# Rotary embedding, one core: the first tile's load cut into eight strided transfers

What was changed: tile 0 arrives in eight transfers instead of two, each of every eighth partition with one 64 KB run per DMA engine; and the load of tile 2 is split 10 and 6 rows around the first store instead of 8 and 8.

## Chip, cores, metric

One core of one Trainium2 chip. The metric is device time in microseconds. For a single core a lone run is reported with the state "unknown"; where that is so, I say so.

## The reference, cut

```python
x: (16, 512, 16, 64) float32   # batch, seq, heads, dim: 33.55 MB
cos, sin: (512, 32) float32
x1, x2 = x[..., :32], x[..., 32:]
first  = x1[..., :16] * cos[..., :16] - x1[..., 16:] * sin[..., :16]
second = x1[..., :16] * sin[..., :16] + x1[..., 16:] * cos[..., :16]
out = concatenate([first, second, x2], -1)
```

Half of each row is rotated and half is only copied. Everything is read once and written once: 67.1 MB.

## The kernel before

Four tiles of 8.39 MB, each [128 partitions x 16 rows x 4 KB], so 64 KB per partition, pass through a ring of three buffers. VectorE rotates in place; loads and stores are issued by the sync engine in program order.

```python
K = 16; NS = 3; KC = K // 2; K0 = K // 4
ring = const_pool.tile([P, NS, K, H, D], fp32)

def rows(t, lo, hi):
    return ring[:, t % NS, lo:hi].rearrange("p k h d -> p (k h d)")
def load(t, lo=0, hi=K):
    nc.sync.dma_start(out=rows(t, lo, hi), in_=xf[t, :, lo * R : hi * R])
def store(t, lo=0, hi=K):
    nc.sync.dma_start(out=of[t, :, lo * R : hi * R], in_=rows(t, lo, hi))

# cos and sin: two small loads on GpSimd's queue    [cut]
load(0, 0, K0)
load(0, K0, K)
load(1)
load(2, 0, KC)
# four copies that build the tables on VectorE       [cut]
def rotate(t, lo, hi):
    # mul (b = x1*s), mul (x1 = x1*c), sub, add      [cut]

rotate(0, 0, K0)
rotate(0, K0, (K0 + K) // 2)
rotate(0, (K0 + K) // 2, K)
store(0)
load(2, KC, K)
load(3)                       # same buffer as tile 0: waits for store(0)
for t in range(1, T):
    rotate(t, 0, KC)
    rotate(t, KC, K)
    store(t)
```

Of the kernel before, what the change touches and what calls it, by code (L numbers as in the profile page):

```python
# [1 line left out]

# [4 lines left out]


@with_exitstack
def kernel(  # L10
    ctx: ExitStack,
    tc: tile.TileContext,
    x: bass.AP,
    cos: bass.AP,
    sin: bass.AP,
    out: bass.AP,
):
    nc = tc.nc
    fp32 = mybir.dt.float32
    P = 128  # L20
    B, S, H, D = x.shape
    Q = D // 4
    HF = D // 2



    K = 16
    T = B * S // (P * K)
    PB = S // K
    REP = P // PB  # L30
    R = H * D
    NS = 3
    KC = K // 2
    K0 = K // 4

    xf = x.rearrange("b s h d -> (b s h d)").rearrange("(t p f) -> t p f", t=T, p=P)
    of = out.rearrange("b s h d -> (b s h d)").rearrange("(t p f) -> t p f", t=T, p=P)
    cosf = cos.rearrange("(p k) j -> p (k j)", k=K)
    sinf = sin.rearrange("(p k) j -> p (k j)", k=K)

    const_pool = ctx.enter_context(tc.tile_pool(name="const", bufs=1))
    b_pool = ctx.enter_context(tc.tile_pool(name="bp", bufs=1, space=bass.MemoryType.PSUM))


    ring = const_pool.tile([P, NS, K, H, D], fp32)
    stage = const_pool.tile([PB, 2, K, HF], fp32)
    table = const_pool.tile([P, 2, K, 2, Q], fp32)
# [9 lines that stand above are left out]

    nc.gpsimd.dma_start(out=stage[:, 0].rearrange("p k j -> p (k j)"), in_=cosf)  # L58
    nc.gpsimd.dma_start(out=stage[:, 1].rearrange("p k j -> p (k j)"), in_=sinf)  # L59
    load(0, 0, K0)  # L60
    load(0, K0, K)
    load(1)
    load(2, 0, KC)


    for r in range(REP):
        nc.vector.tensor_copy(  # L67
            out=table[r * PB : (r + 1) * PB].rearrange("p t k c j -> p (t k) c j"),
            in_=stage.rearrange("p t k j -> p (t k) j")[:, :, 0:Q]
            .unsqueeze(2)  # L70
            .to_broadcast((PB, 2 * K, 2, Q)),
        )
    C = table[:, 0].rearrange("p k c j -> p k (c j)")
    Sn = table[:, 1].rearrange("p k c j -> p k (c j)")

    def rotate(t, lo, hi):
        n = hi - lo
        x1 = ring[:, t % NS, lo:hi, :, 0:HF]
        c = C[:, lo:hi].unsqueeze(2).to_broadcast((P, n, H, HF))
        s = Sn[:, lo:hi].unsqueeze(2).to_broadcast((P, n, H, HF))  # L80
        b_full = b_pool.tile([P, KC, H, HF], fp32, name="b_t")
        b_t = b_full[:, 0:n]
        nc.vector.tensor_mul(out=b_t, in0=x1, in1=s)  # L83
        nc.vector.tensor_mul(out=x1, in0=x1, in1=c)  # L84
        nc.vector.tensor_sub(  # L85
            out=x1[:, :, :, 0:Q], in0=x1[:, :, :, 0:Q], in1=b_t[:, :, :, Q:HF]
        )
        nc.vector.tensor_add(  # L88
            out=x1[:, :, :, Q:HF], in0=x1[:, :, :, Q:HF], in1=b_t[:, :, :, 0:Q]
        )  # L90

    rotate(0, 0, K0)
    rotate(0, K0, (K0 + K) // 2)
    rotate(0, (K0 + K) // 2, K)
    store(0)
    load(2, KC, K)
    load(3)
    for t in range(1, T):
        rotate(t, 0, KC)
        rotate(t, KC, K)  # L100
        store(t)


# [1 line left out]
_INS = ['x', 'cos', 'sin']  # L105
_OUTS = [((16, 512, 16, 64), 'float32')]


# [23 lines left out]
```

## Time and profile before

| | before |
|---|---|
| median (3 runs, 161.78 to 161.93) | 161.9 us |
| span of the profiled run | 160.1 us |
| hardware DMA queue busy, share of 16 engines | 97.8% |
| VectorE busy | 69% |
| mean rate | 420 GB/s |
| one 64 KB run on one DMA engine | 2.418 us |

A "run" in this document is the contiguous stretch that one DMA engine moves for one partition. The trace has a record of each run with start and duration; no view prints them, so where I quote run times they come from these records. A record names no engine: that a run belongs to this or that engine is inferred from one run's end meeting the next one's start. The tables by stage stand beside them as a rough check: they count a run with all its bytes in the stretch in which it starts, so a share can exceed 1 and a rate be too high where runs cross the end of a stretch. The prediction below shows the views themselves.

### The profile page before, as it was taken

To read this page: it belongs to the slowest core of one execution; us is meant where nothing else is said; L and a number is where in the kernel's file an instruction comes from. 1 tells how busy PE (TensorE), PEld (TensorE's weight loads), DVE (VectorE), ACT (ScalarE), POOL (GpSimd) and SP (SyncE) were. 2 spreads that over 40 slices of the span, in tenths; PEclk is the share of its full clock that TensorE was granted. 3 is DMA by queue.
4 is the path that set the end of the run, shared out by engine and by line. 5 is a ranking of instruction groups with operands and counts; after the bars stand their busy time and mean duration, and the time that the engine had idled before them with its cause. 6 is when DMAs were issued, how large, how long until landed. Compare 5 with 4: busy or idle time off the path is not lost.

```text
span 160.1 us, 109 instructions
## 1 busy us (share of the span) xinstructions
DVE 110.0 (69%) x40; POOL 1.3 (1%) x6
## 2 busy tenths in 40 slices
DVE  0069709999999999999999994799999900000000
POOL 3000000000000000000000000000000000000000
DMA  6999999699699799899996996996996996996991
GB/s 197 385 504 454 393 459 524 262 524 491 295 401 581 328 524 409 377 393 418 483 540 295 491 524 262 524 524 262 524 524 262 524 524 262 524 491 295 524 459 66
DMA packets 1504, 67.24 MB, mean 420 GB/s; under 512 B 192, under 2 KB 192, under 8 KB 224
## 3 DMA queue, kind: packets, MB, share of 16 engines
q1 hardware_dynamic: 1440, 67.11, 97.8%
q0 software_dynamic: 64, 0.13, 0.2%
HBM read 33.69 MB, written 33.55 MB: 420 GB/s over the span
## 4 chain that ended last, share of the span: by engine, by line
DMA 50%; DVE 28%; DVEq 1%; issue 0%; SPq 0%
DMA ring<-in_x_dram 32%; DMA out_dram<-ring 18%; DVE b_t L83 10%; DVE ring L84 10%; DVE ring L85 5%; DVE ring L88 3%; DVEq L127 1%; SPq L53 0%; DVEq L83 0%
## 5 line engine op out<-in xcount | busy, mean ns | idle before, releaser
L83 DVE TENSOR_TENSOR b_t<-ring,table 128x4096 f32<-128x4096 f32 (+2 forms) x9 | 35.6, 3959 | 8.2 <-DMA ring<-in_x_dram 8.0
L84 DVE TENSOR_TENSOR ring<-ring,table 128x4096 f32<-128x4096 f32 (+2 forms) x9 | 35.6, 3950 | 0.3
L85 DVE TENSOR_TENSOR ring<-ring,b_t 128x2048 f32<-128x2048 f32 (+2 forms) x9 | 18.4, 2049 | 0.3
L88 DVE TENSOR_TENSOR ring<-ring,b_t 128x2048 f32<-128x2048 f32 (+2 forms) x9 | 18.4, 2042 | 0.0
L67 DVE COPY table<-stage 32x1024 f32<-32x1024 f32 x4 | 2.7, 684 | 9.2 <-DMA stage<-in_sin_dram 9.1
L58 POOL DMA_DIRECT2D stage<-in_cos_dram x1 | 0.6, 631 | 0.8 <-PEq L127 0.8
L59 POOL DMA_DIRECT2D stage<-in_sin_dram x1 | 0.5, 498 | 0.0
L116 POOL MEMSET const-bfloat16-1.0<- 128x1 bf16 x1 | 0.1, 102 | 0.0
L116 POOL MEMSET const-float32-0.0<- 128x1 f32 x1 | 0.1, 99 | 0.2 <-issue 0.2
L116 POOL MEMSET const-float32-1.0<- 128x1 f32 x1 | 0.1, 99 | 0.0
L116 POOL MEMSET const-uint8-127<- 128x1 uint8 x1 | 0.1, 99 | 0.0
## 6 DMA issues: line engine op xcount, KB each, us to landing
ring<-in_x_dram SPq DMA_DIRECT2D x2, 4096.0 KB, 43.9
ring<-in_x_dram SPq DMA_DIRECT2D x1, 6144.0 KB, 22.4
ring<-in_x_dram SPq DMA_DIRECT2D x1, 2048.0 KB, 8.5
stage<-in_cos_dram POOLq DMA_DIRECT2D x1, 64.0 KB, 6.0
stage<-in_sin_dram POOLq DMA_DIRECT2D x1, 64.0 KB, 7.2
out_dram<-ring SPq DMA_DIRECT2D x4, 36.4
ring<-in_x_dram SPq DMA_DIRECT2D x2, 35.0
```

The lines of the kernel that those rows point to most:

```text
L58: nc.gpsimd.dma_start(out=stage[:, 0].rearrange("p k j -> p (k j)"), in_=cosf)
L59: nc.gpsimd.dma_start(out=stage[:, 1].rearrange("p k j -> p (k j)"), in_=sinf)
L67: nc.vector.tensor_copy(out=table[r * PB : (r + 1) * PB].rearrange("p t k c j -> p (t k) c j"), in_=stage.rearrange("p t k j -> p (t k) j" ...
L83: nc.vector.tensor_mul(out=b_t, in0=x1, in1=s)
L84: nc.vector.tensor_mul(out=x1, in0=x1, in1=c)
L85: nc.vector.tensor_sub(out=x1[:, :, :, 0:Q], in0=x1[:, :, :, 0:Q], in1=b_t[:, :, :, Q:HF])
L88: nc.vector.tensor_add(out=x1[:, :, :, Q:HF], in0=x1[:, :, :, Q:HF], in1=b_t[:, :, :, 0:Q])
L116: nc = _bacc.Bacc("TRN2", target_bir_lowering=False, num_devices=1)
L127: with _tile.TileContext(nc) as tc:
```

## The change

Its intent is presumably to bring every DMA engine to 64 KB runs at once and to give each transfer all 16 engines. VectorE can then not start on the first four rows, and the 10/6 split keeps the queue filled until the later first store.

```diff
-    K0 = K // 4
+    K2 = 10
+    G = 8
...
-    load(0, 0, K0)
-    load(0, K0, K)
+    for g in range(G):
+        nc.sync.dma_start(
+            out=ring[:, 0].rearrange("(e g) k h d -> g e (k h d)", g=G)[g],
+            in_=xf[0].rearrange("(e g) f -> g e f", g=G)[g],
+        )
     load(1)
-    load(2, 0, KC)
+    load(2, 0, K2)
...
-    rotate(0, 0, K0)
-    rotate(0, K0, (K0 + K) // 2)
-    rotate(0, (K0 + K) // 2, K)
+    rotate(0, 0, KC)
+    rotate(0, KC, K)
     store(0)
-    load(2, KC, K)
+    load(2, K2, K)
```

The scratch tile of `rotate` is also allocated at its exact size; every piece is now 8 rows, so this changes nothing. The order of instructions on VectorE differs only by the missing third piece of tile 0.

More of the change, by code (lines that the diff above doesn't have):

```diff
@@ L80, in rotate @@
         s = Sn[:, lo:hi].unsqueeze(2).to_broadcast((P, n, H, HF))
-        b_full = b_pool.tile([P, KC, H, HF], fp32, name="b_t")
-        b_t = b_full[:, 0:n]
-        nc.vector.tensor_mul(out=b_t, in0=x1, in1=s)
+        b_t = b_pool.tile([P, n, H, HF], fp32, name="b_t")
+        nc.vector.tensor_mul(out=b_t[:], in0=x1, in1=s)
         nc.vector.tensor_mul(out=x1, in0=x1, in1=c)
```

## The prediction

In the prediction the sum of the forecast came to 161.9 + 19.3 - 0.9 = 180.3 us: the time before; 19.3 us because the eight runs of tile 0 on each engine were to take twice their 2.418 us, 4.84; and 0.9 us less for the tidying and the start. The doubling was my supposition, no trace of the kernel before showed it. "It" in "Nothing downstream gives it back" and "the 19.3" are this term. Rival A is tile 0 at half rate, B is tile 0 at full rate.

> **What bounds the kernel now.** I read the page first (engine busy shares, slices, DMA queues), then the chain of waits, then the sync engine's own waits, then a table of stages.
>
> ```profile
> DVE 110.0 (69%) x40; POOL 1.3 (1%) x6
> q1 hardware_dynamic: 1440, 67.11, 97.8%
> q0 software_dynamic: 64, 0.13, 0.2%
> HBM read 33.69 MB, written 33.55 MB: 420 GB/s over the span
> ring<-in_x_dram SPq DMA_DIRECT2D x1, 6144.0 KB, 22.4
> ring<-in_x_dram SPq DMA_DIRECT2D x1, 2048.0 KB, 8.5
> ```
>
> The hardware DMA queue is busy for 97.8% of all 16 engines' span, VectorE for 69%. So the bound is bytes through the DMA engines: 33.55 MB in, 33.55 MB out. The chain that ended last names VectorE for 28%, and that misleads: while the chain follows VectorE from 23.66 to 44.14 us, the DMA engines are working off loads already queued, and nothing is lost.
>
> The first stage of the timeline and the table by stage:
>
> ```profile
> 11.94 2.30 DVE L83 TENSOR_TENSOR b_t<-ring,table 128x2048 f32<-128x2048 f32 x1
> ...
> 23.66 3.37 DVE L83 TENSOR_TENSOR b_t<-ring,table 128x3072 f32<-128x3072 f32 x1 [4.71 <-DMA ring<-in_x_dram]
> ...
> 44.14 0.35 SPq L56 DMA_DIRECT2D out_dram<-ring  x1
> ```
>
> ```profile
> 0.00:1.75 1.75, 0.00 (x0) 0.70 (x5) 1.00 0.00 0
> 1.75:8.30 6.55, 0.00 (x0) 0.63 (x2) 1.00 1.14 408
> 8.30:22.90 14.60, 9.68 (x8) 0.00 (x0) 1.00 1.04 450
> 22.90:158.60 135.70, 100.33 (x32) 0.00 (x0) 1.00 0.99 427
> 158.60:160.10 1.50, 0.00 (x0) 0.00 (x0) 1.00 0.00 0
> ```
>
> Columns of the second fence: stretch, its length, busy time of VectorE and GpSimd, clock, DMA share, GB/s. The first byte moves at 1.75 us, the last at 158.6, and in between there is no hole.
>
> The trace also holds one record per DMA run, which no view prints. A 64 KB run takes 2.418 us on its engine (27.1 GB/s; 16 engines give 433.6 GB/s), a 48 KB run 1.82 us, a 32 KB run 1.21 us. A 16 KB run takes 0.611 us when undisturbed, but 1.0 to 1.5 us as the first of its engine. Each engine carries 64 times 64 KB: 64 x 2.418 = 154.8 us. From 1.75 to 158.6 are 156.9 us, so all inefficiency of the stream together is 2.1 us. Nearly all of it lies in tile 0, whose last run ends at 23.1 us: 23.1 - 1.75 = 21.35 us against 8 x 2.418 = 19.34.
>
> [...]
>
> [...] each table is a transfer of only 32 partitions, and the 64 software-queue packets are, per table, 16 packets of 4,096 B (two 2 KB rows[...]) and 16 semaphore writes. The 1440 hardware packets are 10 transfers x (128 runs + 16 semaphore writes)[...].
>
> [...]
>
> [...]
>
> [...]
>
> **The change part by part.**
>
> *Bytes, VectorE, tables.* The same 67.1 MB. VectorE loses one group of four operations: tile 0 went in 4+6+6 rows, now 8+8. Before: 2.30 + 2.29 + 1.22 + 1.21 and twice 3.37 + 3.36 + 1.75 + 1.75, together 27.5 us. After: twice 4.43 + 4.42 + 2.29 + 2.28, together 26.8. VectorE can no longer start on 4 rows at 11.94 but waits for the whole tile. With tile 0 down at about 22.5 it would be rotated at 22.5 + 26.8 = 49.3 us instead of 44.14.
>
> *The 10/6 split.* It pays for that. Queued ahead of the first store are now 8 + 8 + 5 = 21 runs of 64 KB per engine, until 1.75 + 1 + 21 x 2.418 = 53.5 us, against 52.2 now. The store issued at 49.3 needs about 1 us to start (0.74 issued, 1.75 first byte, at the start of the span), so 3 us of slack remain. The other end: 6 rows are 6/16 x 19.34 = 7.3 us of transfer between the end of store 0 and the start of load 3, which waits for that store; an issue of about 1 us fits. No bubble at either end: 0 us.
>
> *Eight issues.* Four load issues took 1.88 us of the sync queue, so about 0.45 each; eight take 3.6 us, while one run lasts at least 2.418. The engines stay fed: 0 us. Extra semaphore writes: 7 more per engine at 9 ns, 0.06 us.
>
> *Run length.* 16 + 48 KB become 64 KB: 0.611 + 1.82 = 2.43 against 2.418, times 8: -0.1 us. Of the 2.0 us of excess in tile 0 the first-run latency and the tables' 0.3 us stay; disturbed small runs may go. I estimate -0.8 us.
>
> [...] Nothing downstream gives it back, as every later transfer already runs end to end. Tile 0 would end near 41.5 us, be rotated at 68.3, and the queue would hold work until 41.5 + 13 x 2.418 = 72.9. So no bubble is added to the 19.3 either.
>
> [...]
>
> **The rivals.**
>
> *A, [...]:* 180.3 us (178 to 182). [...]
>
> *B, [...]:* tile 0 runs at full rate and only the tidying remains, 161.9 - 0.8 = 161.1 us (160.4 to 162.5[...]). For it: rate per engine is all the trace shows. After the first table packet the next two 16 KB runs together took about 1.43 us instead of 1.22 on nearly every engine alike[...]. This hints at a cost on the engine's side.
>
> *C, something between:* [...] engines are chosen by partition after all, so that two groups of eight run side by side with the second starting 2 us later. 163 to 174 us.
>
> *D, a new bubble* before store 0 since VectorE starts later: the 3 us of slack speak against it. If the tables came very late (10 us later), VectorE still has them before tile 0 is down.
>
> A gain of over 2% needs 158.7 us. The stream's whole inefficiency is 2.1 us and part of it stays, so that is all but excluded.
>
> **Range and chances.** A gets about 0.62, C 0.06 (most of it beyond 2%), B 0.31. Slower: 0.67, same: 0.32, faster: 0.01. Since A and B lie far apart, a range that holds the time 8 times in 10 has to reach from B's to A's: 160.6 to 182.0 us. The point is A's, 180.3 us, as the likelier one.
>
> **What would show it.** For A: the GB/s of the slices from 4 to 40 us near 215 instead of 440; tile 0's transfers ending one 4.8 us after the other; first multiply at 128x4096 near 41 us; store 0 issued near 68 us; from there on the same spacing of transfers as before (19.35 us per tile), and one 64 KB run of tile 0 about 4.8 us instead of 2.418. For B: first multiply near 22.5 us, store 0 issued near 49.3, last byte near 158. For D: a hole in the DMA row of the slices around 50 us. [...] if runs of tile 0 take 2.42 us, A falls whatever else holds. If they take 4.8 us but the end is less than 17 us later, my claim that nothing downstream gives time back is the faulty step.

## The result

| | before | after |
|---|---|---|
| median | 161.9 us (161.69 to 162.19, 6 runs) | 182.66 us (182.52 to 182.89, 6 runs) |
| span of the profiled run | 160.1 us | 180.9 us |
| last run of tile 0 ends | 23.10 us | 44.04 us |
| last run of the last store ends | 158.6 us | 179.7 us |

The ratio is 1.1283 (95% interval 1.1268 to 1.1297); a ratio here is the mean time of one kernel's fast runs over the mean of the other's of the same rounds, so not quite the ratio of the medians.

The page of the kernel after, engines and queues:

```profile
DVE 109.5 (60%) x36; POOL 1.3 (1%) x6
q1 hardware_dynamic: 1408, 67.11, 97.6%
HBM read 33.69 MB, written 33.55 MB: 372 GB/s over the span
```

The bytes are the same and the queue is as busy as before, 97.6% against 97.8%, but it moves 372 GB/s instead of 420. This is the point to learn from: "busy" counts the time that runs take, and a run that crawls is as busy as one that flies. The shares alone would not say that anything is wrong with the DMA. The page's rate in 40 equal slices of the span does, here before and after:

```profile
GB/s 197 385 504 454 393 459 524 262 524 491 295 401 581 328 524 409 377 393 418 483 540 295 491 524 262 524 524 262 524 524 262 524 524 262 524 491 295 524 459 66
GB/s 232 246 232 174 101 217 217 232 232 232 464 464 464 368 435 435 386 464 464 464 313 435 440 435 464 464 464 464 449 333 391 449 464 464 464 464 449 319 391 232
```

The first ten slices of the second line, 45 us, stay between 101 and 246.

The table by stage of the kernel after (stretch, length, VectorE, GpSimd, clock, DMA share, GB/s):

```profile
2.10:44.10 42.00, 2.73 (x4) 0.27 (x1) 1.00 1.04 226
44.10:179.70 135.60, 106.73 (x32) 0.00 (x0) 1.00 0.98 425
```

All of the loss lies in the first line. Its 226 GB/s and its share of 1.04 include 16 runs of tile 1 that start before 44.10 us; tile 0's own 8.39 MB from 2.10 to 44.04 us are 200 GB/s, against 393 before (1.75 to 23.10 us). From its end on the kernel runs at 425 GB/s, against 427 in the corresponding stretch of before.

The timeline of the kernel after, VectorE's first multiply and the first store:

```profile
0.74 4.99 SPq L63 DMA_DIRECT2D ring<-in_x_dram  x8
...
44.72 4.43 DVE L87 TENSOR_TENSOR b_t<-ring,table 128x4096 f32<-128x4096 f32 x1 [23.16 <-DMA ring<-in_x_dram]
...
71.61 0.35 SPq L57 DMA_DIRECT2D out_dram<-ring  x1
```

VectorE starts at 44.72 us and the store is issued at 71.61 us (the prediction had 41 and 68), while the queue still has loads until 75.6, so no bubble came: the 10/6 split did its part. The eight issues took 4.99 us, not the 3.6 I had worked out, also without harm.

The records of the runs: for g = 0 to 7 a 64 KB run took 4.81, 5.08, 5.06, 5.09, 4.91, 5.11, 5.11 and 5.10 us on the mean of the 16 engines. In the kernel before it takes 2.418. The fifth is a little faster. In e8 below, where two tiles come in this way, the fifth, ninth and thirteenth transfers took 4.93 us a run. What makes them faster is not shown.

### The profile page after: what moved, and what is told of

The parts are those of the page before. It is cut to its first block, busy times and chain, and to the rows that moved or that the text cites. A ratio compares the mean times of both kernels' runs of the same rounds, so it can differ in the third digit from the quotient of the medians.

```text
span 180.9 us, 115 instructions
## 1 busy us (share of the span) xinstructions
DVE 109.5 (60%) x36; POOL 1.3 (1%) x6
## 3 DMA queue, kind: packets, MB, share of 16 engines
q1 hardware_dynamic: 1408, 67.11, 97.6%
## 4 chain that ended last, share of the span: by engine, by line
DVE 54%; DMA 22%; issue 5%; SPq 2%; DVEq 1%
DMA ring<-in_x_dram 22%; DVE b_t L87 20%; DVE ring L88 20%; DVE ring L92 9%; DVE ring L89 6%; SPq L63 2%; DVEq L130 1%; DVEq L87 0%
## 5 line engine op out<-in xcount | busy, mean ns | idle before, releaser
L87 DVE TENSOR_TENSOR b_t<-ring,table 128x4096 f32<-128x4096 f32 x8 | 35.5, 4433 | 23.4 <-DMA ring<-in_x_dram 23.2
L88 DVE TENSOR_TENSOR ring<-ring,table 128x4096 f32<-128x4096 f32 x8 | 35.4, 4425 | 0.3
L89 DVE TENSOR_TENSOR ring<-ring,b_t 128x2048 f32<-128x2048 f32 x8 | 18.3, 2286 | 0.3
L92 DVE TENSOR_TENSOR ring<-ring,b_t 128x2048 f32<-128x2048 f32 x8 | 18.2, 2279 | 0.0
```

What stands on the lines that cost most here:

```text
L87: nc.vector.tensor_mul(out=b_t[:], in0=x1, in1=s)
L88: nc.vector.tensor_mul(out=x1, in0=x1, in1=c)
L89: nc.vector.tensor_sub(out=x1[:, :, :, 0:Q], in0=x1[:, :, :, 0:Q], in1=b_t[:, :, :, Q:HF])
L92: nc.vector.tensor_add(out=x1[:, :, :, Q:HF], in0=x1[:, :, :, Q:HF], in1=b_t[:, :, :, 0:Q])
```

## The experiments

Theories at the start: **P**, the partitions that a transfer covers set its rate: runs that engines move at once to or from certain partitions hold each other up (my supposition). **H**, reading rows 512 KiB apart in HBM is slow. **F**, a small transfer of one run per engine has a fixed cost of about 2.7 us (5.11 - 2.42). All edits below are against the kernel after, unless said otherwise.

| experiment | tile 0's transfers | us per 64 KB run | median us |
|---|---|---|---|
| change | 8 x 16 partitions, step 8 | 5.1 | 182.66 |
| e1 | 1 x 128 | 2.42 | 162.03 |
| e3 | as change, rows together in HBM | 5.1 | 182.5 |
| e5 | 8 x 16, step 2 | 5.1 | 182.71 |
| e4 | 8 x 16, step 1 | 9.3 | 216.77 (one run) |
| e6 | 4 x 32, step 4 | 2.42 | 162.45 |
| e10 | 4 x 32, step 1 | 5.1 | 182.74 (one run) |
| e14 | 2 x 64, step 2 | 2.42 | 162.38 (one run) |
| e15 | 2 x 64, step 1 | 5.1 | 182.79 (one run) |
| e11 | 7 x 16, step 7, and 16 in a block | 3.4 to 4.7; 8.2 (medians by transfer) | 182.73 |

The kernel before took 161.83 to 162.04 us (medians) beside these.

### One transfer for tile 0

```diff
-    for g in range(G): ...        # eight transfers
+    load(0)
```

> Tile 0 arrives in one transfer of 128 partitions, the rest of the change (tile 2 split 10 and 6, halves of 8 rows) stays. All three theories of the loss, P [...], H (rows 512 KiB apart in HBM) and F (a fixed cost of each small transfer), put it into the eight transfers: 161.1 us expected, 160.4 to 162.0. If the rest of the change carried part of the loss, this stays above 163.

162.03 us (161.73 to 162.47, 6 runs) against 161.83; ratio 1.0013 (0.9992 to 1.0034). So the whole loss is in the eight transfers. The rest of the change is worth nothing: my 0.8 us of tidying did not come, and 162.03 is just outside the expected range. The stretch of tile 0, to set against the 226 GB/s of the change:

```profile
1.80:22.90 21.10, 2.73 (x4) 0.57 (x2) 1.00 1.06 441
```

### Only the eight transfers

Against the kernel before:

```diff
-    load(0, 0, K0)
-    load(0, K0, K)
+    for g in range(8): ...        # the eight transfers
```

> The kernel before, with only tile 0's two loads replaced by the eight transfers; tile 2 still split 8 and 8, tile 0 rotated in 4, 6 and 6 rows. P, H and F all expect the loss of the whole change, 182.7 us (182.2 to 183.5). Tile 0 would be rotated near 44.7 + 27.5 = 72.2 us and the queue has work until 44.0 + 12 x 2.418 = 73.0, so with about 1 us to start a store a bubble is just avoided or a few tenths long.

185.45 us (185.13 to 185.67), outside the range: 2.8 us slower than the whole change. The runs of tile 0 are the same (4.86 to 5.12 us), but the loads in the queue ended between 72.55 and 73.24 us and the store was issued at 72.52 and began to move at 73.36, so engines stood idle for 0.1 to 0.8 us. By the records the last runs of the first store and of the load of tile 3 took 3.15 and 3.33 us instead of 2.42 as well, some 1.6 us more; why, I did not test. It shows an idle stretch that the change, with its 10/6 split, does not have; how much of the 2.8 us the split alone is worth, it does not show.

### Near rows in HBM

```diff
-            in_=xf[0].rearrange("(e g) f -> g e f", g=G)[g],
+            in_=xf[0, 16 * g : 16 * g + 16],      # wrong result on purpose
```

> Wrong result on purpose: the eight transfers go to the same partitions 8e+g as in the change, but read 16 rows that lie together in HBM (64 KiB apart instead of 512). P: [...] 182.7 us, a run of tile 0 5.11 us; if the distance in HBM gives the part beyond doubling (5.11 instead of 4.84), 180.5 us and 4.84. H: the loss goes, about 161.5 us and 2.42 a run. F: 182.7 us.

182.5 us, 5.1 us a run. H is out, both as the cause of the loss and as the cause of the part beyond doubling. The 512 KiB pitch costs about 0.2 us (182.66 - 182.5) or nothing.

### Sixteen partitions side by side

```diff
-            out=ring[:, 0].rearrange("(e g) k h d -> g e (k h d)", g=G)[g],
-            in_=xf[0].rearrange("(e g) f -> g e f", g=G)[g],
+            out=ring[16 * g : 16 * g + 16, 0].rearrange("p k h d -> p (k h d)"),
+            in_=xf[0, 16 * g : 16 * g + 16],
```

> Eight transfers of 16 partitions next to each other (16g to 16g+15), rows together in HBM, result right. P: [...] a run takes 9.7 us (4 x 2.418) to 10.2 (twice 5.11), tile 0 ends at 79 to 84 us, the whole 219 to 224 us. H: about 161.5 us. F: as the change, 5.11 us a run and 182.7 us.

216.77 us (one run, state unknown), 9.28 us a run, a little below the range. The table by stage of this run:

```profile
2.00:78.00 76.00, 2.73 (x4) 0.38 (x1) 1.00 0.94 115
78.00:214.00 136.00, 106.74 (x32) 0.00 (x0) 1.00 0.98 424
```

Neighbouring partitions instead of every eighth, and about half the rate again: 115 GB/s instead of 226, or by tile 0's own bytes 111 instead of 200. A fixed cost per transfer (F) cannot do this, as number and size of the transfers are those of the change. A run takes 9.28 / 2.418 = 3.84 times as long as in the kernel before, in the change 5.11 / 2.418 = 2.11 times: near four and two, but not exactly.

### Step 2 instead of step 8

```diff
+        q, b = g // 2, g % 2
-            out=ring[:, 0].rearrange("(e g) k h d -> g e (k h d)", g=G)[g],
-            in_=xf[0].rearrange("(e g) f -> g e f", g=G)[g],
+            out=ring[32 * q : 32 * q + 32, 0].rearrange("(e b) k h d -> b e (k h d)", b=2)[b],
+            in_=xf[0, 32 * q : 32 * q + 32].rearrange("(e b) f -> b e f", b=2)[b],
```

> Eight transfers of 16 partitions with a step of 2 (32q + 2e + b), rows 128 KiB apart in HBM, result right. [...] P: again about double, [...] the whole 178.9 to 182.7 us. H: between 162 and 170 us, as the rows are closer. F fell with the step-1 run (216.8 us).

182.71 us, 5.11 us a run. Other partitions, 2 apart instead of 8, and the same time. It also says that 5.11 us does not need partitions that lie 32 apart in one transfer: here a transfer has none.

### Four transfers of 32 partitions, step 4

```diff
-    for g in range(G):      # and g=G in both rearranges
+    for g in range(4):      # and g=4
```

> Four transfers of 32 partitions, every fourth one (4i+g), so two rows per engine [...]. [...] 162 us. If [...] an engine takes rows 2e and 2e+1 one after the other: [...] 5.1 us a run, about 182.7 us. If rows are dealt out another way (e and e+16): [...] again about 182 us.

162.45 us, 2.42 us a run but for the start and the tables. So it is not the stride over partitions and not the number of transfers. For the two ways of dealing rows to engines that I had named I had expected 182 to 183 us; how the rows are dealt is not in the records, and it stays open.

### Two queues

```diff
+    for i in range(G):
+        g, eng = i // 2 + 4 * (i % 2), (nc.sync, nc.scalar)[i % 2]
+        eng.dma_start(...)        # the same eight transfers
```

> The same eight transfers, issued in turn by the sync queue (g = 0..3[...]) and by ScalarE's queue (g = 4..7[...]). If an engine works one run at a time and all take the two queues in the same order, [...] 180 to 183 us. If each engine keeps a run of either queue in flight or the engines fall out of step, [...] 162 to 166 us, runs that overlap on one engine. P allows either, but only P lets this change anything: the bytes, rows and sizes are the same.

182.0 us (181.78 to 182.31). In the records 16 runs of one queue and 16 of the other follow in turn, 4.9 to 5.2 us each on the mean, so each engine seems to take one run from either queue in turn, all in step. With two queues transfers of g = 0 to 3 and of g = 4 to 7 were on offer at once, and no time was won.

### Tile 1 in eight transfers too

```diff
-    load(1)
+    for g in range(G): ...        # as for tile 0, with ring[:, 1] and xf[1]
```

> Tile 1 comes in eight such transfers as well. P: [...] nothing downstream returns it, so it comes a second time: 8 x (5.11 - 2.42) = 21.5 us more, less some tenths at the seam, 203.5 to 204.5 us. If part of the loss was a start-up cost: under 202. If slack later on returned some: under 202 as well.

231.9 us, far off. The runs of tile 1 took 5.1 us like those of tile 0, and its last run ended at 84.6 us, 40.6 after tile 0's, so the loss did come a second time (40.6 - 19.35 = 21.2 us). Most of the other 28 us is a fault of the experiment, seen in its timeline:

```profile
85.39 4.43 DVE L91 TENSOR_TENSOR b_t<-ring,table 128x4096 f32<-128x4096 f32 x1 [67.69 <-DMA ring<-in_x_dram]
```

VectorE's first multiply on tile 0 waited for tile 1 as well, and by the records no data moved for 9.0 us before the first store, 7.3 us after it and 8.8 us before the last one, 25 us together. As a dose test it is spoiled; the half dose below took its place.

### Step 7

```diff
+    for g in range(7):     # partitions 7e + g of the first 112
+        ...rearrange("(e g) ... -> g e ...", g=7)[g]
+    # one transfer for partitions 112 to 127
```

> Seven transfers of 16 partitions with a step of 7 (7e+g, one 64 KB run per engine as in the change) and an eighth of the 16 partitions left, 112 to 127. [...] P: most runs of these seven take 2.42 us and the few that share 5.1; by my estimate from those two times the last engine is through tile 0 about 29.4 us after the first byte instead of 42, the eighth transfer slow for most: 169 to 173 us in all. If single-run transfers or the stepping over partitions cost time by themselves (what is left of F): 5.1 us for nearly all runs, 182 us or more.

182.73 us (three runs, 182.18 to 183.38; a fourth, 186.14, was slow and is left out), against 169 to 173 expected. P in its simple form falls here: I expected most runs of a transfer at 2.42 us. Instead, in three transfers (g = 0 to 2) nearly every run took about 4.5 us, and in a fourth (g = 4) two runs took 4.44 and the other 14 took 3.4 to 3.6: none was free. The table by stage of this run:

```profile
2.10:32.00 29.90, 2.73 (x4) 0.27 (x1) 1.00 1.03 248
```

What couples the runs is not shown. What remains as a working hypothesis (W): what counts is the set of partitions of the whole transfer, and its runs are slowed together.

### Blocks of 32 partitions

```diff
+    for q in range(4):
+        nc.sync.dma_start(out=ring[32 * q : 32 * q + 32, 0]..., in_=xf[0, 32 * q : 32 * q + 32])
```

> Four transfers of 32 partitions next to each other[...]. The run with 32 partitions at a step of 4 was at full rate[...]. [...] 9.28 us a run as with step 1, 216.8 us. If instead rows 2e and 2e+1 go to one engine, [...] 5.1 us and 182.7 us. [...] 162.5 us.

182.74 us (one run, state unknown), 5.1 us a run: slow, where 32 partitions at a step of 4 (e6) took 2.42, but not 9.28. So the inference about how 32 rows are dealt on which the 9.28 rested was wrong.

### Half the bytes through the eight transfers

```diff
-            # 64 KB runs
+            out=ring[:, 0, 0:KC]..., in_=xf[0, :, 0 : KC * R]...     # 32 KB runs
+    load(0, KC, K)
```

> The eight transfers bring only the first 8 rows of each partition (32 KB runs), the other 8 come in one transfer of 128 partitions. P: half the bytes, so half the loss: 8 x (2.56 - 1.21) = 10.8 us, 172.5 to 173.0 us, a run of the eight 2.56 us. A fixed cost of each transfer: 8 x 2.7 as before, 182 to 184 us, a run 3.9 us.

171.93 us (171.75 to 172.16), a little under the expected range, and 2.54 us a run of 32 KB (1.21 in the kernel before). This is 9.9 us above e1, a little under half of the change's 20.6 (182.66 - 162.03). The loss goes with bytes, not with the number of transfers.

### The last store in eight transfers

Against e1:

```diff
-        store(t)
+        # t == 3: eight transfers, of[t] and ring[:, t % NS] rearranged as tile 0 in the change
```

> Tile 0 comes in one transfer (162.0 us in the first experiment), and the last store goes out in eight transfers with a step of 8 instead. [...] 5.11 us a run and about 183 us. If only writes into SBUF are limited: 162.0 to 163 us, 2.42 a run.

181.12 us (181.07 to 181.58), runs of 3.0 to 5.4 us, most 5.0 to 5.1. Table by stage:

```profile
2.00:139.00 137.00, 109.47 (x36) 0.37 (x1) 1.00 0.99 424
139.00:178.00 39.00, 0.00 (x0) 0.00 (x0) 1.00 0.98 215
```

So a store in pieces of every eighth partition is slowed about as a load is; the whole took 1.9 us less than expected. One rival is left for stores: these rows also lie 512 KiB apart in HBM, and e3 cleared that distance for loads only.

### Eight engines at a time

```diff
+    for i in range(16):
+        q, g = 32 * (i // 4), i % 4
+        # partitions q + 4e + g, e = 0..7: ring[q:q+32, 0] and xf[0, q:q+32], "(e g) ... -> g e ...", g=4, [g]
```

> Sixteen transfers of 8 partitions at a step of 4 (32q + 4i + g, 8 engines, one 64 KB run each)[...]. P: [...] 2.42 us a run; only half the engines work on tile 0, 16 x 2.42 = 38.7 us, the whole near 180 us (179 to 183). F2 (transfers of one run per engine go at half rate[...]): 4.8 to 5.1 us a run, the whole near 220 us. N [...]: the first eight transfers, partitions 0 to 63, 2.42 us a run, the last eight, 64 to 127, slow.

197.81 us (one run, state unknown), not 180; its records are worth a look. Two stretches of this run, tile 0 still loading in both:

```profile
8.00:27.00 19.00, 2.73 (x4) 0.00 (x0) 1.00 0.52 222
28.00:57.00 29.00, 0.00 (x0) 0.00 (x0) 1.00 0.98 206
```

In the first stretch only half the engines work (share 0.52), each run takes 2.42 us and the rate is 222 GB/s. At 26.26 us the sync engine issues the load of tile 1, and the eight idle engines begin it. In the second stretch all 16 work (0.98) and the rate falls to 206. Transfers 8 and 9, partitions 64 to 95 on the first eight engines, had taken 2.42 us a run; transfers 11 to 15, of the same form and also to partitions 64 to 127, now take 5.05 to 5.11, and so do tile 1's runs on the other eight engines. The same engines and the same kind of transfer, alone and then with company: so the engine by itself does not set the time of a run. Nor is company alone enough: in e6 and e14 a run took 2.42 us with all 16 engines at work. That transfers 11 to 15 and tile 1's runs went to partitions that hold each other up is P's reading; which partitions tile 1 was writing at that time the records do not say. F2 is out (single-run transfers reach 2.42), N too, if the same eight engines carried all sixteen transfers, as eight runs at a time, each starting where one ended, suggest: it expected transfers 8 to 15 slow, and 8 and 9 took 2.42. I had missed this collision, and with it the 180 us.

### Two transfers of 64 partitions

```diff
-    for g in range(G):      # step 8, g=G
+    for g in range(2):      # e14: step 2, g=2
```

```diff
+    for q in range(2):      # e15: blocks 64q to 64q+63
+        nc.sync.dma_start(out=ring[64 * q : 64 * q + 64, 0]..., in_=xf[0, 64 * q : 64 * q + 64])
```

> Two transfers of 64 partitions at a step of 2, four runs per engine[...]. W [...]: 2.42 us a run, 162 to 162.6 us. If an engine's rows follow one another and only the moment counts: 5.1 us and 182.7 us.

> Two transfers of 64 partitions next to each other, four runs per engine[...]. W and P: 5.1 us a run, 182.7 us, although these are large transfers of 4 MB with four runs per engine and rows together in HBM. F2: 2.42 us and 162 us. [...]

e14 took 162.38 us and e15 182.79 (one run each, state unknown). Tile 0's stretch, first of e14:

```profile
2.10:23.40 21.30, 2.73 (x4) 0.27 (x1) 1.00 1.05 437
```

then of e15:

```profile
2.10:43.90 41.80, 2.73 (x4) 0.28 (x1) 1.00 1.04 226
```

Both are two transfers of 4 MB with four runs per engine; they differ in which partitions go together. That is a factor of 1.93 in rate (1.96 by tile 0's own bytes, 393 against 201 GB/s). What goes together in one transfer decides. Both times are those expected from W.

## Why the prediction was right or wrong

- **The bound** (bytes through the DMA engines) and **the eight transfers as the place of the loss**: right, e1 took 162.03 us. That it is the partitions of a transfer that count is shown by e6 (2.42 us a run) against e10 (5.1) and by e14 against e15; e3, e4, e12 and e13 each take away one other explanation. Why just these partitions slow each other, no run shows. Rival B (tile 0 at full rate, as the engine sets it) is refuted by the 5.1 us a run, and e13's two stretches speak against it too. Rival C (163 to 174 us) did not come; only the fifth transfer, at 4.91 us, was 0.2 us under 5.11. By e11 (182.73 us against 169 to 173) P as I used it is incomplete: nearly all runs of a transfer were slowed.
- **Nothing downstream gives time back, no new bubble (rival D)**: right. Tile 0 ends 20.94 us later (44.04 - 23.10) and the span is 20.8 longer.
- **The size**: wrong, 182.66 against 180.3 and outside the range that ended at 182.0. Two terms of the sum "161.9 + 19.3 - 0.9" were mis-sized. The first is the step from 2.418 to 4.84 us a run: it supposed exactly twice 2.418. A run took up to 5.11 us; over the eight transfers the mean runs sum to 40.27 us instead of 38.69, 1.6 us more. The second is the tidying of 0.8 to 0.9 us: e1 shows that it is worth nothing (ratio 1.0013). The two together are 2.5 us; the miss is 2.4.
- **The second term in detail.** Without small runs tile 0 does load 0.3 us earlier in e1 (22.82 against 23.10), but the time does not reach the end. In the changed kernel the start was later instead: the 16 engines began at 2.29 us on the mean, against 1.88 before. Its first run of tile 1 also took 2.96 us on the mean instead of 2.42. Of the small terms, the "7 more" semaphore writes are 6 (eight transfers instead of two), which changes 0.01 us.
- **The range.** Its upper end allowed 1.7 us for a term of 19.3 for which no trace gave a rate; only one engine's rate and a supposed doubling stood behind it. Even an allowance of 10% of it, 1.9 us, would have ended at 182.2 and missed.
- **The weight given to rival B**, 0.31, came from the table packets, after which two 16 KB runs took about 1.43 us instead of 1.22 on nearly every engine. After e11, where nearly all runs of a transfer were slowed together (about 4.5 us for g = 0 to 2), this need not be a cost on the engine's side. That remains an interpretation; the table packets were not tried by themselves.

Still open: what makes runs to certain partitions slow each other; why a run takes more than twice 2.418 us in the change (2.11 times) and less than four times in e4 (3.84); what couples the runs in e11; how rows of 32 and 64 partitions are dealt to engines; whether the distance of rows in HBM matters for stores; the slower last runs of two transfers in e2. No version tried beats the kernel before beyond noise.

## What to carry to other kernels

Before cutting a transfer by partitions, write down which partitions each piece takes, and compare with what was measured here. Loads in pieces of 32 partitions at a step of 4 (e6) or 64 at a step of 2 (e14) cost next to nothing, 2.42 us a run (162.45 and 162.38 us in all); pieces of 16 at a step of 8 or 2 (the change, e5) and of 32 or 64 neighbours (e10, e15) ran at about a half, 5.1 us; 16 neighbours (e4) at about a quarter, 9.28 us; and a store in pieces of 16 at a step of 8 (e9) at about a half. A form that is not among these has to be timed: e11 fell outside its range. A DMA queue that is 97% busy may still be crawling (here 97.6% at 372 GB/s, before 97.8% at 420), so compare GB/s stage by stage. And when a term rests on a rate that no trace shows, let the range be as wide as that rate is uncertain.
